# Part of a stream transpose moved from TensorE to VectorE and DMA, split one strip later

## The chip, the cores and the metric

The kernel runs on one core of one Trainium2 chip. The metric is the device time of one execution in microseconds (us), the median of several. The kernel before takes 2370.52 us (median of 3 runs, 2370.17 to 2370.91).

## The reference

Two layers of a causal decoder for 256 tokens with a stream `x` of width 2048, all in f32. Layer 0 has stick-breaking attention, layer 1 dilated window attention over shared keys and values; both have a gated ConvFFN and a gated embedding after it (called ple here):

```python
for i in range(DEPTH):                                  # DEPTH = 2
    h = rms_norm(x, attn_norm_w[i])
    x = x + (mixer_a(h, a_w_qkv, a_w_o) if i == 0 else mixer_b(h, b_w_q, b_w_o, shared K/V))
    x = x + conv_ffn(rms_norm(x, ffn_norm_w[i]), ffn_w_up[i], ffn_conv_w[i], ffn_conv_b[i], ffn_w_down[i])
    gate = sigmoid(rms_norm(x, ple_norm_w[i]) @ ple_w_gate[i])
    x = x + gate * (p[i] @ ple_w_proj[i])
return rms_norm(x, final_norm_w)
```

D_FF is 5632, the attention of layer 0 has 16 heads of 128, that of layer 1 has 12. The shared keys and values come from a norm of the stream between the layers.

## The kernel before

**Products.** Every f32 operand is split in two parts of fewer bits, high and low, and a product is three products: high by high, low by high, high by low. Weights come from memory in pieces of 4 blocks of 128x512 (`raw`, 1 MB, 4 buffers, loaded by SP's queue in order). ScalarE writes the high part of two blocks (`whi`, line 275), VectorE the low part (`wlo`, line 276); there are 4 buffers of each, so they run up to three pairs ahead of TensorE. Both are placed with a high priority.

**The stream** lies in `x[0]`, `x[1]`: 128 tokens each on the partitions, 2048 columns. It is treated in four strips `s` of 512 columns. Five stages end by adding to it strip by strip and preparing the next stage's operand, and are called the five parts here: the output projection of layer 0 (`wo_a`, 16 blocks per strip), the second half of its down projection (`wdn`), its ple, the output projection of layer 1 (`wo_b`, 12 blocks per strip), and the second half of its down projection. In each, TensorE makes a strip's two products of 128 tokens (`strip_v`, lines 317 to 319, tile `accv`), VectorE adds them to the strip (line 565, in ple line 660), and ScalarE squares the result for the next norm (line 212).

**The turn.** The next stage needs the strip with its columns on the partitions, as four blocks of 128x256. `turn(s)` has TensorE transpose it: 8 transposes of 128x128 by the identity (line 244) into two banks (`two`). Then `split_x` writes each block times the norm's gain as `h`: ScalarE the high half (line 140), VectorE the low half (line 141); ple keeps a plain copy too (`xT`, line 672). The first half of each down projection has no norm and no turn, nor has the last ple.

**The norm.** After strip 3 VectorE sums the squares, ScalarE takes ln and exp (lines 164, 165) and VectorE makes a diagonal matrix (`diag`, line 230), which TensorE multiplies by ones (`nrm`, line 232) to spread the factor over columns; after the down projections this last product is left out.

**Memory for the turn's results** comes from a ring of NRING tiles of 128x512, which `h`, `xT`, the FFN's products `g` and the attention's tiles share. The FFN has 11 pairs of up strips; `half` says how many are made, and multiplied by their rows of the down projection, before the rest.

**Order.** Each engine has one queue and takes its instructions in order. A scheduler lays them out at build time by the order of the program and by priorities; `tc.issue_after(i)` keeps what follows on an instruction's engine behind it. POOL (GpSimd) has no work in the program.

Of the kernel before, what the change touches and what calls it, by code (L numbers as in the profile page):

```python
# [10 lines left out]
F32 = mybir.dt.float32  # L11
# [3 lines left out]
AF = mybir.ActivationFunctionType  # L15
# [48 lines left out]

RAW = 4
WARM = 9
NRING, NRAW, NWSP = 42, 4, 4
AHEAD = 200
KV_AT = (0, 6, 12, 16)
PI_PARTS = _two_pi_parts()  # L70
# [3 lines left out]
def tile_trunk(ctx, tc, head_d, xT_d, x_d, pT_d, pos_d, vec_d, cst_d, csb_d, wqkv, wo_a, wkv, wq_b, wo_b, wup, wdn, wpg, wpp, gfin_d, out_d):  # L74
# [3 lines left out]
    wraw = ctx.enter_context(tc.tile_pool(name="wraw", bufs=NRAW))  # L78
    wsp = ctx.enter_context(tc.tile_pool(name="wsp", bufs=NWSP))
    tmp = ctx.enter_context(tc.tile_pool(name="tmp", bufs=3))  # L80
    psum = ctx.enter_context(tc.tile_pool(name="psum", bufs=8, space=bass.MemoryType.PSUM))

    uid = [0]
# [45 lines left out]
    def gain(base, j):  # L129
        return vec[:, base + j : base + j + 1]  # L130


    last = {}

    def split_x(src, j, bases):

        out = []
        for b in bases:
            h = rt("h", dt=F32R)
            last["split"] = nc.scalar.activation(h[:, :S], src, AF.Copy, scale=gain(b, j)).ins  # L140
            nc.vector.scalar_tensor_tensor(  # L141
                h[:, S:], src, gain(b, j), f32(h[:, :S]), op0=OP.mult, op1=OP.subtract
            )
            out.append(h)
        return out

# [4 lines left out]
    def strip_of(t, s):  # L151
        return x[t][:, s * 512 : (s + 1) * 512]
# [51 lines left out]
    class Norm:  # L204
# [4 lines left out]

        def add(self, s, t):  # L210
            q = tt("sq", (P, 768), tag="e", bufs=1)[:, :512]
            nc.scalar.activation(q, strip_of(t, s), AF.Square, accum_out=self.s[:, t, s : s + 1])  # L212

        def half(self, t):

# [20 lines left out]

    def turn(s):

        two = two_banks()
        out = [two[:, o // 2, (o % 2) * S : (o % 2 + 1) * S] for o in range(4)]  # L240
        for o, d in enumerate(out):
            for t in (1, 0):
                c = s * 512 + o * P
                nc.tensor.transpose(d[:, t * P : (t + 1) * P], x[t][:, c : c + P], idf)  # L244
        return two, out

    def weights(W, s, n, fine=False, before=lambda k0: None, block=None, base=0, ringed=0):

# [308 lines left out]
    def add_strips(W, xs, gain_of, norm, base=0):  # L557

        out = []
        for s in range(4):  # L560
            ps = strip_v(W, s, xs, base)
            if norm is not None and s == 3:
                norm.table = load_table()
            for t in range(2):
                nc.vector.tensor_tensor(strip_of(t, s), ps[t], strip_of(t, s), op=OP.add)
                if norm is not None:
                    norm.add(s, t)
            if norm is not None:
                for o, b in enumerate(turn(s)[1]):
                    out += split_x(b, 4 * s + o, [gain_of])  # L570
        return out

    def ffn(i, xs, rstd):
        cv = V_CONV + i * 4 * 2 * FB

        def conv(j, ps, y):
            col = lambda r: vec[:, cv + r * 2 * FB + j : cv + r * 2 * FB + j + 1]
            u = tt("u", tag="t", bufs=6)
            evac(ps, rstd, u)
            nc.scalar.activation(y, u, AF.Identity, scale=col(2), bias=col(3))  # L580
            nc.vector.scalar_tensor_tensor(y[:, 1:], u[:, : S - 1], col(1), y[:, 1:], op0=OP.mult, op1=OP.add)
            nc.vector.scalar_tensor_tensor(y[:, 2:], u[:, : S - 2], col(0), y[:, 2:], op0=OP.mult, op1=OP.add)

        def part(strips):
            gs = []
            for s in strips:
                ps = strip_t(wup[i], s, xs)
                gates = []
                for o in range(4):
                    y = tt("gate", bufs=4)  # L590
                    conv(4 * s + o, ps[o], y)
                    silu = nc.scalar.activation(y, y, AF.Silu).ins
                    gates.append(y)
                ps = strip_t(wup[i], FB // 4 + s, xs)
                for o in range(4):
                    y = tt("val", tag="t", bufs=6)
                    conv(FB + 4 * s + o, ps[o], y)
                    nc.vector.tensor_tensor(y, y, gates[o], op=OP.mult)
                    g = rt("g", dt=F32R)
                    split(y, g)  # L600
                    gs.append(g)
            return gs, silu

        half = (FB // 4 + 1) // 2
        gs, _ = part(range(half))
        add_strips(wdn[i], gs, None, None)
        gs, silu = part(range(half, FB // 4))
        if i == 0:
            rotary_tables(silu)
        norm = Norm()  # L610
        h = add_strips(wdn[i], gs, G_PLE + i * KB, norm, base=4 * half)
        return h, norm
# [23 lines left out]
    def ple(i, xs, ps_, rc, norm, gain_of=None):  # L636

        out, raw, gf = [], [], []
        if gain_of is None:
            for s in range(4):  # L640
                t = rt("gfin")
                nc.scalar.dma_start(
                    t, bass.AP(tensor=gfin_d.tensor, offset=gfin_d.offset + 512 * s, ap=[[0, P], [1, 512]])
                )
                gf.append(t)
        for s in range(4):
            end = gain_of is None and s == 3
            if end:
                pr = strip_v(wpp[i], s, ps_)
                gp = strip_v(wpg[i], s, xs, tail=KB, ringed=KB // 2)  # L650
            else:
                gp = strip_v(wpg[i], s, xs)
                pr = strip_v(wpp[i], s, ps_)
            for t in range(2):
                g = tt("pg", (P, 768), tag="w", bufs=2)[:, :512]
                nc.scalar.activation(g, gp[t], AF.Sigmoid, scale=rc[:, t : t + 1])
                if s == 3 and (end or t == 1):
                    norm.table = load_table()
                nc.vector.tensor_tensor(g, pr[t], g, op=OP.mult)
                nc.vector.tensor_tensor(strip_of(t, s), strip_of(t, s), g, op=OP.add)  # L660
                norm.add(s, t)
                if end:
                    finish(t, norm.half(t), gf[3])
                elif gain_of is None:
                    nc.vector.tensor_tensor(strip_of(t, s), strip_of(t, s), gf[s], op=OP.mult)
                if end and t == 0:
                    tc.keep_in_program_order(nc.scalar.preload_act_table_set("sigmoid_and_others"))
            if gain_of is not None:
                two, bs = turn(s)
                for o in range(0, 4, 2):  # L670
                    r = rt("xT")
                    nc.scalar.activation(r, two[:, o // 2], AF.Copy)
                    raw += [r[:, :S], r[:, S:]]
                    for q in range(2):
                        out += split_x(bs[o + q], 4 * s + o + q, [gain_of])
        return out, raw


# [137 lines left out]
```

## Time and profile before

| what | value |
|---|---|
| median of 3 runs | 2370.52 us |
| the profiled execution | 2371.05 us |
| its span | 2369.3 us, granted TensorE clock 0.998 |
| TensorE busy | 2355.6 us, 99% |
| VectorE busy | 1564.3 us, 66% |
| ScalarE busy | 1270.5 us, 54% |
| POOL busy | 0.2 us |
| the 16 DMA engines, mean busy share | about 0.53 |

The profile is one execution; the span is from its first to its last instruction, and 1.75 us lie around it. A busy TensorE is counted to the modelled end of each product, so products that overlap count as one; what a product costs in sequence is read from the chain that ended last, where a piece stands with the time by which it moved the chain on. A window's row gives, for a stretch of time, each engine's busy time with its number of instructions, the clock, the DMA engines' share and GB/s.

### The profile page before, as it was taken

The numbers are of one execution on the slowest core, as the hardware profiler recorded it, in microseconds if no ns is written. First come the engines' busy times: TensorE is split into PE (matmuls) and PEld (weight loads), VectorE is DVE, ScalarE is ACT, GpSimd is POOL, SyncE is SP. The second block draws the span as 40 slices with busy tenths as digits, with TensorE's granted clock in tenths as the row PEclk, the third lists the DMA queues.
The fourth block names the chain that finished last, engine by engine and source line by source line (L and its number), as shares of the span: only waits on it lengthen the run. The fifth ranks groups of instructions, "written<-read, shape, count | busy, mean of one in ns | idle before, by whom it ended". The sixth has DMA issues, their size and how long they took to land.

```text
span 2369.3 us, 31206 instructions
## 1 busy us (share of the span) xinstructions
PE 2355.6 (99%) x12258; PEld 2004.3 (85%) x12258; DVE 1564.3 (66%) x2377; ACT 1270.5 (54%) x1826; POOL 0.2 (0%) x4
## 2 busy tenths in 40 slices
PE   9999999999999999999999999999999999999998
PEld 7888888888888888888888888888888888888886
DVE  7566555778764578765567875677776457876555
ACT  6555545656543455654565444565654345555454
POOL 0000000000000000000000000000000000000000
PEclk9999999999999999999999999999999999999999
DMA  8455455555555555555555544555555555555553
GB/s 296 174 179 182 163 178 184 194 187 187 196 187 192 190 196 184 190 194 182 184 187 194 178 147 174 183 184 190 193 183 193 195 196 184 190 192 183 193 204 116
DMA packets 64852, 442.82 MB, mean 187 GB/s; under 512 B 7200, under 2 KB 7616, under 8 KB 12736
## 3 DMA queue, kind: packets, MB, share of 16 engines
q1 hardware_dynamic: 62352, 434.93, 52.8%
q10 hardware_dynamic: 2352, 5.88, 0.8%
q8 instruction: 96, 1.57, 0.3%
q14 instruction: 52, 0.43, 0.0%
HBM read 438.69 MB, written 2.10 MB: 186 GB/s over the span
## 4 chain that ended last, share of the span: by engine, by line
PE 99%; DVE 0%; ACT 0%; DMA 0%; issue 0%; SPq 0%; DVEq 0%
PE acc L302 36%; PE acc L305 18%; PE accv L319 14%; PE accv L317 14%; PE accv L318 14%; PE two L346 2%; PE two L244 1%; PE two L420 0%; DMA raw<-in_wqkv 0%; PE keys L346 0%; PE two L421 0%; ACT whi L275 0%; DVE wlo L276 0%; ACT sq L212 0%; PE nrm L232 0%
## 5 line engine op out<-in xcount | busy, mean ns | idle before, releaser
L276 DVE TENSOR_TENSOR wlo<-raw,whi 128x1024 fp32r<-128x1024 f32 (+1 forms) x821 | 1003.9, 1223 | 722.0 <-ACT whi L275 718.6
L275 ACT ACTIVATE whi<-raw 128x1024 fp32r<-128x1024 f32 (+1 forms) x821 | 868.2, 1058 | 881.7 <-PE accv L319 426.6
L302 PE MATMUL acc<-h,whi 128*128 128x512 f32 x3712 | 1167.0, 396 | 1.9 <-DVE h L141 1.6
L305 PEld LDWEIGHTS acc<-h,wlo 128*128 128x128 f32 x3712 | 697.1, 188 | 163.3
L305 PE MATMUL acc<-h,wlo 128*128 128x256 f32 x3712 | 731.0, 278 | 0.0
L302 PEld LDWEIGHTS acc<-h,whi 128*128 128x128 f32 x3712 | 567.1, 189 | 4.6 <-DVE h L141 1.9
L319 PE MATMUL accv<-whi,g 128*128 128x512 f32 x704 | 274.7, 390 | 0.0
L318 PE MATMUL accv<-wlo,g 128*128 128x512 f32 x704 | 274.2, 390 | 0.0
L317 PE MATMUL accv<-whi,g 128*128 128x512 f32 x704 | 274.1, 389 | 0.0
L317 PE MATMUL accv<-whi,h 128*128 128x512 f32 x464 | 181.8, 392 | 0.0
L319 PE MATMUL accv<-whi,h 128*128 128x512 f32 x464 | 181.4, 391 | 0.0
L318 PE MATMUL accv<-wlo,h 128*128 128x512 f32 x464 | 181.4, 391 | 0.0
L318 PEld LDWEIGHTS accv<-wlo,g 128*128 128x128 f32 x704 | 132.2, 188 | 27.4
L319 PEld LDWEIGHTS accv<-whi,g 128*128 128x128 f32 x704 | 132.2, 188 | 27.2
L317 PEld LDWEIGHTS accv<-whi,g 128*128 128x128 f32 x704 | 132.2, 188 | 27.1
L324 ACT ACTIVATE c<-acc 128x256 f32<-128x256 f32 x232 | 86.4, 374 | 33.4 <-PE acc L305 33.4
L319 PEld LDWEIGHTS accv<-whi,h 128*128 128x128 f32 x464 | 87.2, 188 | 18.0
L317 PEld LDWEIGHTS accv<-whi,h 128*128 128x128 f32 x464 | 87.2, 188 | 17.5
L318 PEld LDWEIGHTS accv<-wlo,h 128*128 128x128 f32 x464 | 87.2, 188 | 17.4
L325 DVE TENSOR_TENSOR c<-acc,c 128x256 f32<-128x256 f32 x232 | 92.2, 418 | 0.0
L319 PE MATMUL accv<-whi,o 128*128 128x512 f32 x224 | 88.0, 393 | 0.0
L318 PE MATMUL accv<-wlo,o 128*128 128x512 f32 x224 | 87.5, 391 | 0.0
(178 smaller groups left out, 1416.9 us busy)
## 6 DMA issues: line engine op xcount, KB each, us to landing
raw<-in_wup SPq DMA_DIRECT2D x176, 1024.0 KB, 4.8
raw<-in_wdn SPq DMA_DIRECT2D x88, 1024.0 KB, 4.8
raw<-in_wqkv SPq DMA_DIRECT2D x44, 1024.0 KB, 4.9
raw<-in_wpg SPq DMA_DIRECT2D x32, 1024.0 KB, 4.9
raw<-in_wkv SPq DMA_DIRECT2D x24, 1024.0 KB, 4.8
raw<-in_wo_a SPq DMA_DIRECT2D x16, 1024.0 KB, 4.8
raw<-in_wq_b SPq DMA_DIRECT2D x12, 1024.0 KB, 4.9
raw<-in_wo_b SPq DMA_DIRECT2D x12, 1024.0 KB, 4.9
```

The lines of the kernel that those rows point to most:

```text
L244: nc.tensor.transpose(d[:, t * P : (t + 1) * P], x[t][:, c : c + P], idf)
L275: last["high"] = nc.scalar.activation(hi[:, c], r, AF.Copy).ins
L276: nc.vector.tensor_tensor(lo[:, c], r, f32(hi[:, c]), op=OP.subtract)
L302: nc.tensor.matmul(ps[o], hi[:, c], xs[k], start=k == 0, stop=False)
L305: nc.tensor.matmul(ps[o][:, S:], lo[:, c], xs[k][:, :S], start=False, stop=k == n - 1)
L317: nc.tensor.matmul(ps[t], xl, hi, start=k == 0, stop=False)
L318: nc.tensor.matmul(ps[t], xh, lo, start=False, stop=False)
L319: nc.tensor.matmul(ps[t], xh, hi, start=False, stop=k == n - 1)
L324: last["copy"] = nc.scalar.activation(c, ps[:, S:], AF.Copy).ins
L325: last["sum"] = nc.vector.tensor_tensor(c, ps[:, :S], c, op=OP.add).ins
L346: run.append(nc.tensor.matmul(*args, skip_group_check=True, **kw).ins)
```

## The change

`turn(s)` no longer uses TensorE. VectorE transposes the strip's two tiles in blocks of 32x32 (line 250 of the new kernel) into ring tiles `y`. POOL's queue writes each to a tile in memory (`there`, 256 KB each), waits for both, and reads them back in four DMAs (line 257, 32 partitions each, pieces of 512 bytes) so that each block lies whole in `z` (name `turned`, one buffer in SBUF). `Turned.add` keeps strips 0 to 2 back: a strip's blocks are split only after the next strip has been added and squared. Strip 3 goes through `turn_at_once`, which is the old `turn`. The splits of strips 0 to 2 now read SBUF in place of PSUM, and ple's plain copies are 16 of 128x256 in place of 8 of 128x512. The ring has 40 tiles in place of 42, and `half` is 5 in place of 6, so that the first half of the down projection has 20 blocks and the second 24.

```diff
--- before.py
+++ after.py
@@ -64,7 +64,7 @@
 
 RAW = 4
 WARM = 9
-NRING, NRAW, NWSP = 42, 4, 4
+NRING, NRAW, NWSP = 40, 4, 4
 AHEAD = 200
 KV_AT = (0, 6, 12, 16)
 PI_PARTS = _two_pi_parts()
@@ -78,6 +78,7 @@
     wraw = ctx.enter_context(tc.tile_pool(name="wraw", bufs=NRAW))
     wsp = ctx.enter_context(tc.tile_pool(name="wsp", bufs=NWSP))
     tmp = ctx.enter_context(tc.tile_pool(name="tmp", bufs=3))
+    dram = ctx.enter_context(tc.tile_pool(name="dram", bufs=2, space=bass.MemoryType.DRAM))
     psum = ctx.enter_context(tc.tile_pool(name="psum", bufs=8, space=bass.MemoryType.PSUM))
 
     uid = [0]
@@ -132,15 +133,18 @@
 
     last = {}
 
+    def like(ap, src):
+        return ap.rearrange("p (a r) -> p a r", r=src.shape[2]) if len(src.shape) == 3 else ap
     def split_x(src, j, bases):
 
         out = []
         for b in bases:
             h = rt("h", dt=F32R)
-            last["split"] = nc.scalar.activation(h[:, :S], src, AF.Copy, scale=gain(b, j)).ins
-            nc.vector.scalar_tensor_tensor(
-                h[:, S:], src, gain(b, j), f32(h[:, :S]), op0=OP.mult, op1=OP.subtract
-            )
+            high, low = like(h[:, :S], src), like(h[:, S:], src)
+            last["split"] = nc.scalar.activation(high, src, AF.Copy, scale=gain(b, j)).ins
+            nc.vector.scalar_tensor_tensor(low, src, gain(b, j), f32(high), op0=OP.mult, op1=OP.subtract)
             out.append(h)
         return out
 
@@ -209,7 +213,8 @@
 
         def add(self, s, t):
             q = tt("sq", (P, 768), tag="e", bufs=1)[:, :512]
-            nc.scalar.activation(q, strip_of(t, s), AF.Square, accum_out=self.s[:, t, s : s + 1])
+            square = nc.scalar.activation(q, strip_of(t, s), AF.Square, accum_out=self.s[:, t, s : s + 1])
+            last["square"] = square.ins
 
         def half(self, t):
 
@@ -236,13 +241,47 @@
 
     def turn(s):
 
+        there = dram.tile([2 * P, 512], F32, tag="turn", name=nm("there"))
+        for t in range(2):
+            y = rt("y")
+            nc.vector.transpose(
+                y.rearrange("p (b o r) -> p o b r", b=4, o=4), strip_of(t, s).rearrange("p (o b c) -> p o b c", o=4, b=4)
+            )
+            nc.gpsimd.dma_start(there[t * P : (t + 1) * P], y)
+        z = tt("turned", (P, 8, 4, 32), bufs=1)
+        back = there.rearrange("(a c) (b f) -> b c a f", c=32, b=4)
+        for b in range(4):
+            nc.gpsimd.dma_start(z[32 * b : 32 * b + 32].rearrange("p a o r -> p a (o r)"), back[b])
+        return [z[:, :, o] for o in range(4)]
+    def turn_at_once(s):
         two = two_banks()
         out = [two[:, o // 2, (o % 2) * S : (o % 2 + 1) * S] for o in range(4)]
         for o, d in enumerate(out):
             for t in (1, 0):
                 c = s * 512 + o * P
                 nc.tensor.transpose(d[:, t * P : (t + 1) * P], x[t][:, c : c + P], idf)
-        return two, out
+        return out
+    class Turned:
+        def __init__(self, use):
+            self.use = use
+            self.strip = None
+        def add(self, s):
+            if self.strip is not None:
+                with tc.issue_after(last["square"]), tc.issue_after(last["added"]):
+                    self.use(*self.strip)
+            if s == 3:
+                self.use(s, turn_at_once(s))
+            else:
+                self.strip = (s, turn(s))
 
     def weights(W, s, n, fine=False, before=lambda k0: None, block=None, base=0, ringed=0):
 
@@ -557,17 +596,22 @@
     def add_strips(W, xs, gain_of, norm, base=0):
 
         out = []
+        def use(s, blocks):
+            for o, b in enumerate(blocks):
+                out.extend(split_x(b, 4 * s + o, [gain_of]))
+        turned = Turned(use)
         for s in range(4):
             ps = strip_v(W, s, xs, base)
             if norm is not None and s == 3:
                 norm.table = load_table()
             for t in range(2):
-                nc.vector.tensor_tensor(strip_of(t, s), ps[t], strip_of(t, s), op=OP.add)
+                last["added"] = nc.vector.tensor_tensor(strip_of(t, s), ps[t], strip_of(t, s), op=OP.add).ins
                 if norm is not None:
                     norm.add(s, t)
             if norm is not None:
-                for o, b in enumerate(turn(s)[1]):
-                    out += split_x(b, 4 * s + o, [gain_of])
+                turned.add(s)
         return out
 
     def ffn(i, xs, rstd):
@@ -601,7 +645,7 @@
                     gs.append(g)
             return gs, silu
 
-        half = (FB // 4 + 1) // 2
+        half = FB // 4 // 2
         gs, _ = part(range(half))
         add_strips(wdn[i], gs, None, None)
         gs, silu = part(range(half, FB // 4))
@@ -636,6 +680,17 @@
     def ple(i, xs, ps_, rc, norm, gain_of=None):
 
         out, raw, gf = [], [], []
+        def use(s, blocks):
+            for o, b in enumerate(blocks):
+                if o % 2 == 0:
+                    r = rt("xT")
+                d = r[:, o % 2 * S : (o % 2 + 1) * S]
+                nc.scalar.activation(like(d, b), b, AF.Copy)
+                raw.append(d)
+                out.extend(split_x(b, 4 * s + o, [gain_of]))
+        turned = Turned(use)
         if gain_of is None:
             for s in range(4):
                 t = rt("gfin")
@@ -657,7 +712,7 @@
                 if s == 3 and (end or t == 1):
                     norm.table = load_table()
                 nc.vector.tensor_tensor(g, pr[t], g, op=OP.mult)
-                nc.vector.tensor_tensor(strip_of(t, s), strip_of(t, s), g, op=OP.add)
+                last["added"] = nc.vector.tensor_tensor(strip_of(t, s), strip_of(t, s), g, op=OP.add).ins
                 norm.add(s, t)
                 if end:
                     finish(t, norm.half(t), gf[3])
@@ -666,13 +721,7 @@
                 if end and t == 0:
                     tc.keep_in_program_order(nc.scalar.preload_act_table_set("sigmoid_and_others"))
             if gain_of is not None:
-                two, bs = turn(s)
-                for o in range(0, 4, 2):
-                    r = rt("xT")
-                    nc.scalar.activation(r, two[:, o // 2], AF.Copy)
-                    raw += [r[:, :S], r[:, S:]]
-                    for q in range(2):
-                        out += split_x(bs[o + q], 4 * s + o + q, [gain_of])
+                turned.add(s)
         return out, raw
 
 
```

TensorE's queue at the start of `wo_a`'s strip 1, before (accv: the products; o: attention's output; x, idf: the transposes' operands):

```order
L317 MATMUL accv_2783<-whi_2779,o_784 128x512 [waits Activation_49]
L318 MATMUL accv_2783<-wlo_2780,o_784 128x512 [waits DVE_49]
L319 MATMUL accv_2783<-whi_2779,o_784 128x512
L317 MATMUL accv_2783<-whi_2779,o_787 128x512
L318 MATMUL accv_2783<-wlo_2780,o_787 128x512
L244 MATMUL two_2756<-idf,x_75 128x128 [waits DMAHW3_49,DMAHW2_49,DVE_49]
L244 MATMUL two_2756<-idf,x_74 128x128 [waits DMAHW5_49]
```

and now:

```order
L356 MATMUL accv_2776<-whi_2772,o_786 128x512 [waits Activation_49]
L357 MATMUL accv_2776<-wlo_2773,o_786 128x512 [waits DVE_49]
L358 MATMUL accv_2776<-whi_2772,o_786 128x512
L356 MATMUL accv_2776<-whi_2772,o_789 128x512
L357 MATMUL accv_2776<-wlo_2773,o_789 128x512
L358 MATMUL accv_2776<-whi_2772,o_789 128x512
L356 MATMUL accv_2783<-whi_2772,o_786 128x512
```

Eight transposes (two are shown) stood between the fifth product and the sixth and waited for VectorE's additions; they are gone. In the whole queue 12012 products and transposes stand where there were 12132.

ScalarE's queue in `wo_b` where strip 2 has just been added, before (sq: the squares; h: the splits; whi: the weights' high parts):

```order
L212 ACTIVATE sq_12928,ssum_12560<-x_74 128x512 [waits DVE_49]
L212 ACTIVATE sq_12931,ssum_12560<-x_75 128x512 [waits DVE_49,Activation_49]
L140 ACTIVATE h_12942<-two_12933,vec 128x256 [waits PE_49]
L140 ACTIVATE h_12945<-two_12933,vec 128x256 [waits DVE_49]
L275 ACTIVATE whi_13026<-raw_13024 128x1024 [waits DMAHW4_49,PE_49]
L140 ACTIVATE h_12948<-two_12933,vec 128x256 [waits DVE_49]
L275 ACTIVATE whi_13042<-raw_13024 128x1024 [waits PE_49]
```

and now:

```order
L216 ACTIVATE sq_12959,ssum_12597<-x_76 128x512 [waits DVE_49]
L216 ACTIVATE sq_12962,ssum_12597<-x_77 128x512 [waits DVE_49,Activation_49]
L314 ACTIVATE whi_13060<-raw_13058 128x1024 [waits DMAHW4_49,PE_49]
L146 ACTIVATE h_12964<-turned_12849,vec 128x256 [waits DMASW6_49,DMASW7_49,DMASW1_49,DMASW0_49]
L146 ACTIVATE h_12967<-turned_12849,vec 128x256
L146 ACTIVATE h_12970<-turned_12849,vec 128x256
L146 ACTIVATE h_12973<-turned_12849,vec 128x256
L314 ACTIVATE whi_13076<-raw_13058 128x1024 [waits PE_49]
```

The splits are now those of strip 1, their first waits for four DMAs of POOL's queue in place of TensorE, and the last `whi` of strip 3's weights stands behind them all.

ScalarE's queue where `wo_a` ends, before (n: ln and exp of the norm; two: strip 3's blocks):

```order
L212 ACTIVATE sq_3247,ssum_2611<-x_74 128x512 [waits DVE_49]
L212 ACTIVATE sq_3250,ssum_2611<-x_75 128x512 [waits DVE_49,Activation_49]
L140 ACTIVATE h_3261<-two_3252,vec 128x256 [waits PE_49]
L164 ACTIVATE n_3275<-rcol_3273 128x2 [waits DVE_49]
L165 ACTIVATE n_3275<-n_3275 128x2 [waits Activation_49]
L140 ACTIVATE h_3264<-two_3252,vec 128x256 [waits DVE_49]
```

and now:

```order
L216 ACTIVATE sq_3246,ssum_2613<-x_76 128x512 [waits DVE_49]
L216 ACTIVATE sq_3249,ssum_2613<-x_77 128x512 [waits DVE_49,Activation_49]
L146 ACTIVATE h_3251<-turned_3101,vec 128x256 [waits DMASW6_49,DMASW7_49,DMASW1_49,DMASW0_49]
L146 ACTIVATE h_3254<-turned_3101,vec 128x256
L146 ACTIVATE h_3257<-turned_3101,vec 128x256
L314 ACTIVATE whi_3399<-raw_3397 128x1024 [waits DMAHW6_49,PE_49]
L146 ACTIVATE h_3260<-turned_3101,vec 128x256
L146 ACTIVATE h_3272<-two_3263,vec 128x256
L168 ACTIVATE n_3286<-rcol_3284 128x2 [waits DVE_49]
L169 ACTIVATE n_3286<-n_3286 128x2 [waits Activation_49]
```

Strip 2's four splits and one `whi` now stand ahead of the norm's ln and exp. The product `nrm` that waits for this norm stands on TensorE's queue behind 38 products of the next stage where it stood behind 22. At the end of `wo_b` the order is the other way round: ln and exp stand right behind the squares, ahead of strip 2's splits, and `nrm` stands behind 19 products where it stood behind 22. At the end of layer 0's ple the splits stand ahead, and 46 products lie between strip 3's transposes and `nrm` where 18 lay.

POOL's queue had no rows of the program; now it has six DMAs for each of the 15 turns of strips 0 to 2. The two writes wait for VectorE's transposes; the first of the four reads waits for both writes, and for ScalarE to be done with the blocks that `turned` held before.

## The prediction

> **What bounds the kernel now.** I read the page first, then the chain that ended last, in order of time, then the busy time of each engine in the stretch with the shortest strips, then the DMA issues and the waits. The page:
>
> ```profile
> span 2369.3 us, 31206 instructions
> PE 2355.6 (99%) x12258; PEld 2004.3 (85%) x12258; DVE 1564.3 (66%) x2377; ACT 1270.5 (54%) x1826; POOL 0.2 (0%) x4
> PEclk9999999999999999999999999999999999999999
> PE 99%; DVE 0%; ACT 0%; DMA 0%; issue 0%; SPq 0%; DVEq 0%
> PE acc L302 36%; PE acc L305 18%; PE accv L319 14%; PE accv L317 14%; PE accv L318 14%; PE two L346 2%; PE two L244 1%; PE two L420 0%; DMA raw<-in_wqkv 0%; PE keys L346 0%; PE two L421 0%; ACT whi L275 0%; DVE wlo L276 0%; ACT sq L212 0%; PE nrm L232 0%
> ```
>
> TensorE is the chain from end to end at its full clock. Nothing else ends a wait that matters, so what TensorE no longer does comes off the time, as long as nothing new makes it wait. The transposes (L244) are 1% of the chain. In order of time the chain shows each group of eight (start us, us by which it moved the chain on); I quote one row for each of the five parts and all three of ple, whose rows differ:
>
> ```profile
> 331.39 0.87 PE two L244 x8
> 1049.23 0.87 PE two L244 x8
> 1161.67 0.88 PE two L244 x8
> 1186.62 0.99 PE two L244 x8
> 1212.14 0.98 PE two L244 x8
> 1475.42 0.90 PE two L244 x8
> 1492.69 0.90 PE two L244 x8
> 2177.06 0.87 PE two L244 x8
> ```
>
> **The change: what leaves TensorE.** Of 20 groups, 15 go. The other two strips of `wo_a` and of both down projections read 0.87 like the row shown, and `wo_b`'s third 0.90. The sum is 3 x 0.87 + 3 x 0.87 + (0.88 + 0.99 + 0.98) + 3 x 0.90 + 3 x 0.87 = 13.4 us. The timeline has a group's modelled length, which overlaps its neighbours:
>
> ```profile
> 1049.06 1.04 PE L244 MATMUL two<-idf,x 128*128 128x128 f32 x8
> ```
>
> So 15 x 1.04 = 15.6 us bounds the gain from above. I take 13.4, because the chain counts what the next product really waits.
>
> **What VectorE gets.** Thirty transposes of 128x512, SBUF to SBUF. No such row exists. The nearest are an addition of the same size with both inputs in SBUF, the fastest instruction of that size, and a shuffle beside an arithmetic instruction of its size:
>
> ```profile
> L660 DVE TENSOR_TENSOR x<-x,pg 128x512 f32<-128x512 f32 x16 | 10.9, 686 | 0.1
> L633 DVE TENSOR_SCALAR x<-x,rhalf 128x512 f32<-128x512 f32 x4 | 1.8, 482 | 0.1
> L401 DVE STREAM_SHUFFLE sw<-qk 32x256 f32<-32x256 f32 x24 | 9.9, 434 | 0.0
> L402 DVE TENSOR_TENSOR sw<-sw,rot 32x256 f32<-32x256 f32 x24 | 9.7, 404 | 0.0
> L276 DVE TENSOR_TENSOR wlo<-raw,whi 128x1024 fp32r<-128x1024 f32 x819 | 1002.5, 1224 | 722.0 <-ACT whi L275 718.6
> ```
>
> A shuffle costs what arithmetic does, so I take 0.69 us each, 21 us in all. The bounds are 0.48 us, and twice 0.686, 1.37 us, if the data passes twice. All of it lies beside TensorE if VectorE has room in the shortest strips, those of `wo_b`. The windows (length, TensorE, weight loads, VectorE, ScalarE, POOL, clock, DMA share, GB/s):
>
> ```profile
> 1475.00:1492.00 17.00, 17.00 (x80) 14.06 (x79) 10.05 (x13) 8.89 (x15) 0.00 (x0) 1.00 0.53 181
> ```
>
> 10.05 + 2 x 0.69 = 11.4 us (12.8 at the upper bound) in a strip that will last 17.27 - 0.90 = 16.4 us: room, so no cost. If that cover went, the lateness would show as TensorE waiting for `wlo`.
>
> **What ScalarE gets.** 60 splits read SBUF and not PSUM, and ple copies 16 small blocks for 8 large ones:
>
> ```profile
> L140 ACT ACTIVATE h<-two,vec 128x256 fp32r<-128x256 f32 x80 | 37.1, 464 | 10.2 <-DVE h L141 10.0
> L140 ACT ACTIVATE h<-x,vec 128x256 fp32r<-128x256 f32 x14 | 6.3, 495 | 0.0
> L672 ACT ACTIVATE xT<-two 128x512 f32<-128x512 f32 x8 | 4.7, 590 | 0.4 <-PE two L244 0.3
> L148 ACT ACTIVATE p<-pin 128x256 fp32r<-128x256 f32 x4 | 1.4, 400 | 0.0
> ```
>
> 60 x 0.031 + 16 x 0.400 - 8 x 0.590 = 3.5 us more, beside TensorE in an engine busy 8.9 us of 17. No cost. `half` 5 for 6 and the shorter ring leave the number of products as it is; a ring tile that is not yet free only stops `g`, which follows the last product of the strip anyway. No cost either.
>
> **The trip through memory.** This is the new wait: ScalarE's first split of a strip waits for four DMAs, and behind it in its queue stand `whi` rows that TensorE needs. I set a budget at `wo_b`. T is the end of a strip. VectorE then has 3 `wlo`, 4 low halves and 2 transposes in its row order, 3 x 1.224 + 4 x 0.482 + 2 x 0.69 = 7.0 us, with some 0.7 us of waiting for ScalarE T + 7.7. ScalarE asks for the blocks no earlier than after the next strip's squares, about T + 18, so a trip of 10 us holds nobody up. The last `whi` of strip 3 stands behind the splits. TensorE wants it five pairs into that strip (a pair is 12 products of 0.227, 2.72 us), at T + 16.4 + 13.6 = T + 30, and 4 splits, a `whi` and a `wlo` take 4.3 us. So TensorE waits only if the trip is longer than 30 - 4.3 - 7.7 = 18 us. The other parts' strips are longer: `wo_a` 22.7 us (23 us of trip allowed), ple 25.5 (26), `wdn` 28.1 (29). No DMA of POOL's is in this trace; the nearest rows are those of the other queues with the same 256 KB, and the time that SP needs to issue one (ns, min/median/max):
>
> ```profile
> out<-x SPq DMA_DIRECT2D x4, 256.0 KB, 2.7
> out<-x ACTq DMA_DIRECT2D x4, 256.0 KB, 3.0
> pin<-in_pT ACTq DMA_DIRECT2D x2, 256.0 KB, 2.6
> x<-in_xT SPq DMA_DIRECT2D x7, 256.0 KB, 6.6
> L634 SPq DMA_DIRECT2D out<-x x4: 332/360/415, 2353.2 to 2364.4; - x4
> ```
>
> Lower bound: write 2.7, read 2.6, five issues of 0.36: 7.1 us. Upper: 3.0 + 6.6 + five issues that each first wait for a running `wlo`, 5 x (0.36 + 1.22): 17.5 us. I take about 9.5 (2.7 + 5.0 + 1.8), as the write is the very shape of `out`. Within the bounds it costs TensorE nothing. [...]
>
> **The traffic.** Each turn writes and reads 0.52 MB, 15.7 MB in all, in 256 pieces of 2 KB and 1024 of 512 bytes:
>
> ```profile
> DMA packets 64852, 442.82 MB, mean 187 GB/s; under 512 B 7200, under 2 KB 7616, under 8 KB 12736
> q10 hardware_dynamic: 2352, 5.88, 0.8%
> ```
>
> A packet of q10 (2.5 KB on average) takes 0.008 x 16 x 2369 / 2352 = 0.129 us. At that price a turn takes 1280 x 0.129 / 16 = 10.3 us of each DMA engine, where `wo_b` leaves 0.47 x 17.2 = 8.1 us free and the other parts 10.6 or more; ours average 0.8 KB, so I take two thirds of it, which fits everywhere. No cost; late next would be the loads of `raw`.
>
> **The ends of the parts.** The wait there is of the norm's product:
>
> ```profile
> PEld nrm L232 <- DVE diag L230: 1.0, 2, 0.5
> ```
>
> At the end of `wo_a` four splits (2.0 us) and a `whi` (1.06) now stand ahead of ln and exp, and `nrm` stands 16 products later (8 of 0.23, 8 of 0.12: 2.8 us). The wait grows by 0.3 us. In ple's end 28 products more cover the longer chain, and at `wo_b`'s end the chain comes first, as before. Cost: 0.3 us, from 0 to 1.
>
> **The sum** against the profiled execution: 2371.05 - 13.4 + 0.3 = 2357.9. The median lies 0.53 us under that execution: **2357.4 us**.
>
> **Rivals.** (a) *The trip is late and the kernel slower.* Above 18 us TensorE waits in two strips of `wo_b`, above 23 in two of `wo_a`, above 26 in ple. At 24 us, 2 x 6 + 2 x 1 = 14 us eat the gain; at 26 us, 16 + 6 = 22 us make 2379. For it: POOL's issues are in no row, and VectorE, busy 59% here, may hold them up. Against: even with a whole `wlo` ahead of each issue the trip is 17.5 us. [...]
>
> (b) *The gain is hidden.* TensorE would wait for loads instead. This needs 0.143 us a packet: 11.4 us a turn, 3 x 3.3 in `wo_b`, 3 x 0.8 in `wo_a`, 12.5 us together, and 2370. For it: more than a thousand small packets a turn. Against: 0.129 us for packets three times as large, and four `raw` buffers of 5.4 us each in front.
>
> (c) *The norm's wait takes its place*: 3.1 us at each of three ends, if the splits go ahead and TensorE's queue gives no cover, 2357.4 + 9 = 2366. Against: the order covers 2.8 and 4.9 us at two and puts the chain first at the third.
>
> **Chances.** Forecast 0.68; (a) 0.12, of which 0.10 slower than before; (b) 0.10; (c) 0.10. A measurement can tell 0.2% (4.7 us) from no change. Faster: 0.68 + 0.10 + 0.02 = 0.80; within 0.2%: 0.10; slower: 0.10. The range goes from the bound of 15.6 us with the norm's waits gone (2354) to rival (c) (2366).
>
> **What would show it.** Right: the first-half strips of `wo_b` 16.3 to 16.4 us apart in the chain, 5 groups of eight transposes left, no row of TensorE waiting for `whi` or `wlo`, VectorE's transposes near 0.69 us and busy time up by 21, `h` never waiting for a DMA of `turned`. Wrong: `whi` or `h` of ScalarE waiting for `turned`, TensorE idle behind it in `wo_b`; `raw` landing much later than 4.9 us; `nrm` waiting several us; or a longer time around the span, 1.75 us now, from one more queue.

## The result and the profile after

The changed kernel takes 2358.26 us (median of 4 runs, 2357.20 to 2358.42), the kernel before 2370.72 in the same comparison (4 runs, 2370.17 to 2370.92). The ratio is 0.9947, 95% interval 0.9930 to 0.9964. That is 12.5 us less; the forecast was 13.1. The profiled execution took 2358.29 us, so 1.8 us lie outside its span, as before.

The page of the changed kernel: span, busy time of the engines, share of the chain.

```profile
span 2356.5 us, 31193 instructions
PE 2342.1 (99%) x12138; PEld 1992.0 (85%) x12138; DVE 1578.5 (67%) x2407; ACT 1270.9 (54%) x1834; POOL 52.4 (2%) x94
PE 98%; DVE 1%; ACT 0%; DMA 0%; issue 0%; SPq 0%; DVEq 0%; ACTq 0%
```

TensorE lost 120 instructions (15 groups of 8) and 2355.6 - 2342.1 = 13.5 us of busy time. Its idle time went from 2369.3 - 2355.6 = 13.7 us to 2356.5 - 2342.1 = 14.4. So the span is 13.5 - 0.7 = 12.8 us shorter. TensorE is still the chain from end to end.

The added work and what is left of the old, by line (count, busy us, mean ns, idle time ahead and what ended it), and then from the page the DMAs (count, KB each, median us from issue to landing) and POOL's queue (packets, MB, share of 16 engines):

```profile
L250 DVE STREAM_TRANSPOSE y<-x 128x512 f32<-128x512 f32 x30 | 21.1, 702 | 0.0
L146 ACT ACTIVATE h<-turned,vec 128x256 fp32r<-128x256 f32 x60 | 27.1, 495 | 7.4 <-DMA turned<-there 7.4
L267 PE MATMUL two<-idf,x 128*128 128x128 f32 x40 | 5.2, 273 | 0.0
```

```profile
there<-y POOLq DMA_DIRECT2D x30, 256.0 KB, 3.9
turned<-there POOLq DMA_DIRECT2D x60, 128.0 KB, 4.5
raw<-in_wo_b SPq DMA_DIRECT2D x12, 1024.0 KB, 4.8
q0 software_dynamic: 5280, 15.73, 2.3%
```

A VectorE transpose takes 0.70 us. Five groups of TensorE transposes are left. ScalarE did wait for `turned`, 7.4 us in all. The loads of `raw` land as early as before (4.8 us).

Where ScalarE waited is read from `wo_b`, strip by strip. First VectorE (start us, us; the additions L610 start when a strip's products end), then POOL, then ScalarE (in brackets the idle time ahead and what ended it):

```profile
1482.01 1.28 DVE L610 TENSOR_TENSOR x<-accv,x 128x512 f32<-128x512 f32 x2
1490.38 0.70 DVE L250 STREAM_TRANSPOSE y<-x 128x512 f32<-128x512 f32 x1
1498.33 1.28 DVE L610 TENSOR_TENSOR x<-accv,x 128x512 f32<-128x512 f32 x2
1509.09 0.70 DVE L250 STREAM_TRANSPOSE y<-x 128x512 f32<-128x512 f32 x1
1514.65 1.28 DVE L610 TENSOR_TENSOR x<-accv,x 128x512 f32<-128x512 f32 x2
```

```profile
1491.37 0.56 POOL L253 DMA_DIRECT2D there<-y  x1 [1.16 <-DVE y L250]
1497.67 2.34 POOL L257 DMA_DIRECT2D turned<-there  x4 [5.75 <-ACT whi L314]
```

```profile
1505.21 1.71 ACT L146 ACTIVATE h<-turned,vec 128x256 fp32r<-128x256 f32 x4 [2.62 <-DMA turned<-there]
1524.39 1.71 ACT L146 ACTIVATE h<-turned,vec 128x256 fp32r<-128x256 f32 x4 [4.77 <-DMA turned<-there]
```

The strips are 16.3 us apart. The second strip ended at 1482.0. Its second transpose ended at 1491.1 (9.1 us later), its splits began at 1505.2: a trip of 14.1 us. It is made of 0.3 us to the issue, 0.56 of issue, 5.7 until POOL goes on to the reads (it waits for the second write's landing; the `whi` that the row names has no part in the trip), 2.34 for four issues, and 5.2 until the last landing. Why the second write took 5.7 us shows in SP's queue. A load of weights of 1 MB was issued 0.9 us ahead of it:

```profile
1490.48 5.57 SPq L297 DMA_DIRECT2D raw<-in_wup  x2
```

The `wlo` between the two transposes frees a `raw` buffer, and the load that then starts landed at 1496.4, the write at 1497.1. The median of 3.9 us above hides this: outside ple the first writes of a trip landed in 2.4 to 2.7 us (one in 3.7), and the second ones, each 0.9 us behind a load, in 5.0 to 6.8.

The third strip's second transpose ended 11.5 us after the strip, since in VectorE's order they stand behind the low halves, and these waited for the late splits. Its splits began 26.1 us after the strip.

Waits of the norm's product:

```profile
PEld nrm L237 <- DVE diag L235: 1.3, 3, 0.6
PE nrm L237 <- DVE diag L235: 0.3, 1, 0.3
```

### The profile page after: what moved, and what is told of

It is laid out like the page before. It is cut to its first block, busy times and chain, and to the rows that moved or that the text cites. A ratio compares the mean times of both kernels' runs of the same rounds, so it can differ in the third digit from the quotient of the medians.

```text
span 2356.5 us, 31193 instructions
## 1 busy us (share of the span) xinstructions
PE 2342.1 (99%) x12138; PEld 1992.0 (85%) x12138; DVE 1578.5 (67%) x2407; ACT 1270.9 (54%) x1834; POOL 52.4 (2%) x94
## 3 DMA queue, kind: packets, MB, share of 16 engines
q0 software_dynamic: 5280, 15.73, 2.3%
## 4 chain that ended last, share of the span: by engine, by line
PE 98%; DVE 1%; ACT 0%; DMA 0%; issue 0%; SPq 0%; DVEq 0%; ACTq 0%
PE acc L341 36%; PE acc L344 18%; PE accv L357 14%; PE accv L356 14%; PE accv L358 14%; PE two L385 2%; PE two L459 0%; DVE wlo L315 0%; DMA raw<-in_wqkv 0%; ACT whi L314 0%; PE keys L385 0%; PE two L460 0%; ACT sq L216 0%; PE two L267 0%; PE nrm L237 0%
```

## The experiments

Each ratio is against runs of the kernel before on the same chip. Its medians were 2370.40 (first four runs), 2370.45 (next four) and 2370.64 (last three).

### Only the removal, only the addition

`no_trip`: the changed kernel, `turn` returns the stream strip itself.

```
     def turn(s):
-        there = dram.tile(...)
...
-        return [z[:, :, o] for o in range(4)]
+        return [strip_of(o // 2, s)[:, (o % 2) * S : (o % 2 + 1) * S] for o in range(4)]
```

> Left out: the trip, and with it the transposing of the first three strips of each part. The splits read the stream strips as they stand, one strip later as in the changed kernel; VectorE's 30 transposes and POOL's 90 DMAs are gone. Theory (what leaves TensorE is the whole gain and the added work is hidden): the time of the changed kernel, 2358.3 us, within 0.5 us, with the same waits for the norm. Rival (the added work costs something, so the gain came out 0.6 us below the forecast): 2357.4 or less.

Measured: 2356.54 us (2356.15 to 2358.94), ratio 0.9942 (0.9929 to 0.9956). That is 13.9 us less than before, where the forecast had 13.4 leaving TensorE. By the letter the rival won: without the trip the kernel is faster than with it. How much is best read beside `hop1` (below), measured on the same chip and the changed kernel in all but one DMA that delays nobody: 2357.38, so 0.8 us. When the starts of the same TensorE products are compared in the traces of the changed kernel and of `no_trip`, 0.6 us of the difference arises between 1519 and 1541 us, around the end of `wo_b`, and 0.5 us in the program's first 15 us, where other pairs of executions differ by as much. So the added work costs 0.6 to 0.8 us, and its place is the end of `wo_b`, where the forecast had only "as before". It is not the trip alone: in `no_trip` the scheduler also put the norm's product there later in TensorE's queue (1522.6 us against 1519.9).

`work_alone`: the kernel before with all its TensorE transposes, and `turn`'s new body beside them, its result unread.

```
     def turn(s):
+        if s < 3:
+            ship(s)
         two = two_banks()
```

> The kernel before with all of its TensorE transposes, and the added work beside them with nobody reading its result: 30 VectorE transposes, 90 DMAs of POOL's queue, the ring of 40 tiles and the down projection's halves as in the changed kernel. Theory (VectorE, the DMA engines and POOL have room): 2370.7 us, the time before, within 0.7 us. Rival of contention (a tenth of the packets' price and late loads): up to 2380; each DMA issue stretched by VectorE would show as a landing and an issue time longer than in the changed kernel.

Measured: 2370.65 us (2370.42 to 2371.53), ratio 1.0002 (0.9993 to 1.0010). Its page and DMA rows:

```profile
PE 2355.9 (99%) x12258; PEld 2003.8 (85%) x12258; DVE 1577.7 (67%) x2407; ACT 1271.3 (54%) x1826; POOL 52.4 (2%) x94
there<-y POOLq DMA_DIRECT2D x30, 256.0 KB, 4.3
turned<-there POOLq DMA_DIRECT2D x60, 128.0 KB, 5.7
```

VectorE's 30 transposes, 16 MB written and read back, and POOL's 90 DMAs cost nothing when nobody waits for them. The removal alone gives the gain; the traffic does not take it back. Rival (b) falls.

### A longer trip

`hop1` and `hop2` put one or two small DMAs between writes and reads; `far1` one that needs the second write. TensorE's order is the same in all three as in the changed kernel; in `far1` a `whi` and its `wlo` changed places with splits in two spots of `wo_b`.

```
+        for _ in range(2):       # hop1: 1
+            nc.gpsimd.dma_start(z[:1, 0], there[:1, :P]...)
...
+            nc.gpsimd.dma_start(z[:1], there[2 * P - 2 :]...)   # far1
         for b in range(4):
             nc.gpsimd.dma_start(z[32 * b : 32 * b + 32]..., back[b])
```

> The changed kernel, with one small DMA (512 bytes, memory to the first row of turned) put between the writes and the reads of each trip, so that the trip is longer by one DMA's latency and nothing else moves. The trip measured from the end of the second transpose to the first split is 14.1 us in wo_b's second strip; with some 4 us more it is 18, the edge of the budget that the prediction gave (18 us). Theory: 2358.3 to 2360 us, TensorE waiting at most 1 us in a strip of wo_b. If the budget was too generous (splits that come late make the next trip later, since VectorE's transposes stand behind the low halves): 2362 or more already.

Measured: 2357.38 us (2357.08 to 2357.76). The dose was almost none: the small DMA reads the first write's rows and runs while the second write lands, and the splits of `wo_b`'s second strip begin at 1505.01 (1505.21 in the changed kernel). Only 2 of the 15 trips got clearly longer (by 3.3 and 7.3 us, in `wo_a` and ple), and nobody waited for these.

> The same with two such DMAs one after the other: a trip of some 22 us. By the prediction's budget TensorE waits 4 us in each of two strips of wo_b and nowhere else (wo_a has 23 us, ple 26, the down projections 29): 2366 us. If the lateness is handed on from strip to strip: 2370 or more, with waits in wo_a too. If TensorE has more in hand than the budget says: 2358.3.

Measured: 2363.57 us (2362.02 to 2367.42), 6.2 us above `hop1`. ScalarE's waits, and those of TensorE, between 1500 and 1545 us (total, times, longest):

```profile
ACT h L146 <- DMA turned<-there: 13.7, 2, 7.1
PE two L269 <- DVE x L612: 1.9, 1, 1.9
```

The splits of the second strip begin at 1509.30, 17.6 us behind its second transpose: 3.5 us more than in the changed kernel, not 8, because only the last of the four reads waited for the small DMAs. TensorE does not wait for `whi` in the strips, where the budget put the loss; once, in the fourth strip of `wo_b`, it waits 0.6 us for a `wlo`. It waits for VectorE's addition `x` at the end of `wo_b`, which stands behind the low halves and transposes of the strip before, for the norm at the end of `wo_a` (1.3 us), and some 25 us into the next part for a `c` (1.8 us).

> The changed kernel with one small DMA (4 KB) between writes and reads that needs the second write, so that every read comes one landing later. A trip of 14.1 us from the end of the second transpose to the first split becomes about 19. By the prediction's budget (18 us) TensorE waits 1 us in each of two strips of wo_b: 2360 us. By the budget corrected with the traces (blocks are asked for on the way at 9 and 11 us behind the strip's end and not 7.7, and each late strip makes the next one later) some 3 to 5 us in each of wo_b's strips and nothing elsewhere: 2367 to 2374.

Measured: 2362.95 us (2362.34 to 2365.52). In `wo_b` the trip grew by less than meant: it is 15.1 and 15.8 us against 14.1 and 14.6. At the third strip of `wo_a` it grew by more: the last read landed 16.2 us after the second transpose, against 12.9 in the changed kernel. The span is 4.7 us longer. By the starts of the same products, 3.6 us are lost at the end of `wo_a` and 2.3 at the end of `wo_b`, and 1.2 were gained in the program's first 15 us, ahead of any turn. POOL's reads of that strip and the first of ScalarE's splits of it, in the changed kernel:

```profile
388.61 2.35 POOL L257 DMA_DIRECT2D turned<-there  x4 [5.27 <-ACT whi L314]
398.01 1.30 ACT L146 ACTIVATE h<-turned,vec 128x256 fp32r<-128x256 f32 x3
```

The last read landed at 395.4, so 2.6 us were in hand. The same in `far1` (the last two reads), with ScalarE's ln and exp (`n`), which stand behind these splits:

```profile
392.56 1.16 POOL L259 DMA_DIRECT2D turned<-there  x2 [2.14 <-DMA turned<-there]
398.78 1.31 ACT L146 ACTIVATE h<-turned,vec 128x256 fp32r<-128x256 f32 x3 [1.93 <-DMA turned<-there]
401.70 0.19 ACT L168 ACTIVATE n<-rcol 128x2 f32<-128x2 f32 x1
401.92 0.20 ACT L169 ACTIVATE n<-n 128x2 f32<-128x2 f32 x1
```

The trip was 3.3 us longer, and it began 1.2 us later after the strip's end, because the splits before it had waited 1.1 us. So ScalarE waited 3.3 + 1.2 - 2.6 = 1.9 us, and TensorE behind it. TensorE's wait, and the windows (length, then busy time and instructions of TensorE, weight loads, VectorE, ScalarE, POOL, then the granted clock, DMA share and GB/s):

```profile
PE nrm L237 <- DVE diag L235: 2.1, 1, 2.1
```

```profile
401.44:404.85 3.41, 1.29 (x7) 0.80 (x6) 3.31 (x9) 2.07 (x5) 0.00 (x0) 1.00 0.00 0
404.85:408.26 3.41, 3.41 (x12) 2.88 (x11) 1.22 (x3) 1.85 (x4) 0.00 (x0) 0.50 0.49 175
```

TensorE waited 2.1 us for the norm, and then worked for 3.4 us at half its clock.

So lateness is paid first at the ends of the parts, through the norm and the last addition, and hardly in the strips.

### An earlier start, and none held back

`early`: VectorE's transposes with a high priority, to stand right behind the additions.

```
-            nc.vector.transpose(...)
+            with tc.high_priority(offset=AHEAD):
+                nc.vector.transpose(...)
```

> The changed kernel with VectorE's two transposes put right behind the strip's additions instead of behind three wlo and four low halves. TensorE's order stays but for one product, ScalarE's order stays but for the last part of wo_b. The trip then begins some 3 us after the strip's end and not 9 to 11, the blocks are there at 17 us, and ScalarE never waits for turned. Theory (the trip's lateness costs 0.6 us at the end of wo_b and nothing else): 2357.4 to 2357.9, that is 0.5 to 1 us less than the changed kernel. Rival (VectorE's wlo, two transposes later, make TensorE wait at each strip's start): 2360 or more.

Measured: 2357.21 us (2357.11 to 2358.15), ratio 0.9943 (0.9929 to 0.9956). The waits and DMAs:

```profile
ACT h L146 <- DMA turned<-there: 0.7, 1, 0.7
PE nrm L237 <- DVE diag L235: 0.9, 1, 0.9
```

```profile
there<-y POOLq DMA_DIRECT2D x30, 256.0 KB, 2.7
```

ScalarE's wait fell from 7.4 to 0.7 us, nearly as expected, though the transposes did not come as early as meant: in `wo_b` the second one ends 7.1 us after the strip, where 3 were expected and 9.1 and 11.5 had been. The median landing of a write is 2.7 us and not 3.9: the two transposes now follow each other without a `wlo` between them, so both writes go out ahead of the next load in most trips, and 10 of the 15 second writes landed in 2.6 to 3.0 us. But at the end of `wo_b` two splits and a `wlo` now stand ahead of the norm's ln, and its product waits 0.9 us there. The gain over the changed kernel (0.1 us by the two spans, 0.8 by the medians, each against its own runs of before) is not separated from nothing by these intervals.

`soon`: no strip is held back.

```
-                self.strip = (s, turn(s))
+                self.use(s, turn(s))
```

> The changed kernel without holding a strip back: the splits of a strip's blocks are issued after its own turn. ScalarE asks for them behind some six whi of the next strip, about 11 us after the strip's end, and they come at 23 us; TensorE has four pairs of whi in hand, some 11 us. Theory (one strip later is what hides the trip): TensorE waits about 5 us in each of 15 strips, 2400 to 2450 us. Rival (the trip would be hidden anyway): 2359 or less.

Measured: 2365.62 us, with a wide spread (10 runs, 2357.58 to 2378.34), ratio 0.9983 (0.9969 to 0.9997). The expectation missed by 34 us at least. The scheduler itself puts the splits behind five `whi` of the next strip (four in ple). ScalarE then waits only 0.9 to 5.8 us at a time (29.7 us in 12 places), where the expectation had 12, and four pairs of `whi` are in hand. So its waits reach TensorE in one place only, again the norm at the end of `wo_b`:

```profile
PE nrm L237 <- DVE diag L235: 4.7, 1, 4.7
```

```profile
1524.95:1528.37 3.42, 0.81 (x6) 0.45 (x4) 2.90 (x6) 3.08 (x8) 0.00 (x0) 1.00 0.00 0
1528.37:1531.78 3.41, 1.33 (x4) 1.15 (x5) 3.15 (x9) 1.49 (x3) 0.00 (x0) 0.50 0.60 195
```

So holding a strip back is worth some 7 us here, with less spread; it is not what hides the trip in the strips.

### Another queue

`sp`: `nc.sync` for `nc.gpsimd` in `turn`.

> The changed kernel with the six DMAs of each turn issued by SP and not by POOL, between SP's loads of weights. Theory (POOL's issues are not starved by VectorE): the landings are as with POOL, 3 to 4 us a write and 4 to 5 us a read, SP issues in about 0.36 us instead of 0.57, the trip is some 2 us shorter, and the loads queued behind the waiting reads come 5 us later, which the four raw tiles cover: 2357 to 2359 us. [...] Second rival (the loads behind the reads come too late): 2365 or more, TensorE waiting for whi.

Measured: 2360.81 us (2359.52 to 2361.13), ratio 0.9958 (0.9944 to 0.9971). Its DMAs, and SP's reads in its queue:

```profile
there<-y SPq DMA_DIRECT2D x30, 256.0 KB, 4.0
turned<-there SPq DMA_DIRECT2D x60, 128.0 KB, 5.4
```

```profile
1517.99 1.82 SPq L257 DMA_DIRECT2D turned<-there  x4
```

SP's landings are no shorter than POOL's (3.9 and 4.5). So nothing shows that VectorE, busy 67%, holds back what POOL issues, which was an argument for rival (a). From the second transpose to the last landing the trips of `wo_b` take 13.5 and 12.4 us, against 14.1 and 14.5 with POOL: shorter, as expected. Still `sp` is slower than the changed kernel by about 2.6 us. Its trace loses them in one place, where TensorE waits for `h` of the third strip; ScalarE's rows show why:

```profile
PE acc L341 <- DVE h L147: 2.6, 1, 2.6
```

```profile
1527.73 1.06 ACT L314 ACTIVATE whi<-raw 128x1024 fp32r<-128x1024 f32 x1 [1.72 <-PE acc L341]
1528.69 1.69 ACT L146 ACTIVATE h<-turned,vec 128x256 fp32r<-128x256 f32 x4
```

The blocks had landed at 1525.2. In this run the scheduler put three more `whi` ahead of these splits, and the last of them waits for TensorE itself. So the loss is one of order on ScalarE, not of the queue's landings.

### The last strips too

`all4`: as `early`, and strip 3 goes through memory in every part. `best`: only in the two down projections, with the norm's arithmetic ahead at the end of `wo_b`; `early_norm` is `best` without the last strips. The cut is from `best`; `all4` has no such conditions.

```
-                self.use(s, turn_at_once(s))
+                self.use(s, turn(s) if self.last else turn_at_once(s))
...
+            with tc.high_priority(offset=AHEAD) if ahead else ExitStack():
                 nc.vector.reduce_sum(rc, self.s, axis=mybir.AxisListType.X)
```

> As the run with early transposes, and the last strip of each part goes through memory too: no transposes on TensorE are left. Five groups of 0.87 to 1.04 us leave, 4.6 us. The last strip's blocks are there 17 us after its end, its splits done at 19; TensorE comes to block 12 of the next part's first strip some 17 us after. Theory: it waits 1 to 2 us at most at each of the five ends, and the time is 2354 to 2358.5. Rival (the trip is 14 us only in the mean, and the next part's wlo and splits stand behind it): waits of 5 us, 2370 or more.

Measured: 2364.45 us (2362.52 to 2366.74), ratio 0.9973 (0.9962 to 0.9985). The 4.6 us left and more came back. The costliest place is the end of ple, 6.6 us by the starts of the same products, where the granted clock is 0.50 again, from within one wait of 3.6 us on:

```profile
PE acc L341 <- DVE h L147: 3.6, 1, 3.6
```

```profile
1243.04:1246.45 3.41, 1.46 (x6) 0.62 (x5) 1.23 (x1) 0.39 (x1) 0.59 (x1) 1.00 0.85 180
1246.45:1249.87 3.42, 1.05 (x3) 0.86 (x4) 1.16 (x3) 2.44 (x8) 0.00 (x0) 0.50 0.64 268
```

> As the run with early transposes, but at the end of wo_b the norm's arithmetic (sum, logarithm, exponential, diagonal) is put ahead of two of the four splits and of a wlo that stood before it there. The early run lost 1.3 us against the changed kernel at that one place, where the norm's product waits. Theory: some 0.5 to 1 us of it comes back, 2356.3 to 2357. Rival (the place does not matter, the difference between these runs is the program's start): 2357.2 as the early run.

Measured: 2357.93 us (2357.86 to 2358.48), ratio 0.9947 (0.9934 to 0.9961). At the end of `wo_b` its trace gains 0.5 us on that of `early`, the lower end of what was expected, but its median is 0.7 us longer. The expectation of the time is not borne out; the place is too small to be seen in it.

> As the run before, and the last strip of the two down projections goes through memory too, while wo_a, ple and wo_b keep TensorE for their last strip. Where all last strips went, these two ends alone lost nothing: 0.91 and 0.80 us left TensorE and no wait came, since ple begins with two strips' products per pair and its first strip asks for block 12 late. Theory: 1.7 us less than the early_norm run, 2354.6 to 2355.4, the fastest of all. Rival (the trip at the end of a down projection collides with ple's loads): no change or slower.

Measured: 2357.02 us (2356.35 to 2360.92), ratio 0.9946 (0.9934 to 0.9959). Its median is the lowest of the complete kernels, but by less than these runs tell apart. In its profiled execution (2360.92 us, its slowest) the norm at the end of `wo_b` was late:

```profile
PE nrm L238 <- DVE diag L236: 2.6, 1, 2.6
```

```profile
1522.53:1525.94 3.41, 1.24 (x7) 1.11 (x8) 3.41 (x6) 2.30 (x5) 0.00 (x0) 1.00 0.00 0
1525.94:1529.35 3.41, 3.41 (x13) 2.83 (x12) 0.71 (x2) 1.55 (x3) 0.00 (x0) 0.50 0.79 238
```

Nor was the end of the first down projection free in that execution: ple's first products waited 1.4 us for an `h`. So what the last strips give is put at risk at the part's end: `early`, `best` and the changed kernel stand within 1.2 us of each other.

## Why the prediction came out right, and where it was wrong

**What leaves TensorE: right.** 13.4 us by the chain; the busy time fell by 13.5, and `no_trip` took 13.9 us less. The chain's rows were the right measure, and the modelled length of the timeline (15.6) was too long.

**VectorE and ScalarE: right.** 0.69 us a transpose was forecast and 0.70 measured, 495 ns a split from SBUF forecast and measured, and no cost where the result is unread (`work_alone`). VectorE's busy time rose by 14.2 us and not by 21: its other instructions took 4.6 us less together in this execution, and overlaps with neighbours count once.

**The traffic: right in the outcome, wrong in the count.** The 5280 packets of q0 are 352 a turn and not 1280 (256 of 4096 bytes and 96 of 4); pieces of 512 bytes did not stand as packets of their own. A packet took 0.023 x 16 x 2356.5 / 5280 = 0.164 us, so a turn took 352 x 0.164 / 16 = 3.6 us of each DMA engine, a third of the 10.3 that the prediction bounded. A packet's price was above the 0.143 us from which rival (b) was to decide; the rival failed by the number of packets.

**The trip: the step that was mis-sized.** The forecast was 9.5 us, the measurement 14.1 and 14.6, inside the bounds of 7.1 to 17.5. The write's landing was put at 2.7 us, from writes at the program's end, and took 5.7 until POOL went on, because a load of 1 MB stood ahead of the second write; the first writes did land in about 2.5. The five issues took 0.56 and 0.59 us each, 2.9 together, where SP's 0.36 had given 1.8. The reads' 5.0 was close (5.2).

**The budget: wrong, and by luck without effect.** It gave 18 us and a margin of 8.5. Its start was T + 7.7; it was 9.1 and 11.5. The sum left out the strip's own two additions (1.28 us), which stand first on VectorE, and a late split makes the next strip's transposes late, which the prediction had not followed around. And it asked the wrong wait: it followed ScalarE's `whi` to TensorE, while lateness first reaches TensorE through the norm's ln and exp and through VectorE's last addition, at the ends of the parts. There little was in hand: 2.6 us at the end of `wo_a`, and none in `wo_b`, where the trip was already waited for. Trips 3.3 and 1.1 us longer lost 3.6 and 2.3 us at these two places (`far1`). "`h` never waiting for `turned`" was wrong too: 7.4 us, hidden.

**The norm: sign right, place wrong.** 0.3 us at the end of `wo_a` was forecast and `wo_b` left unchanged. TensorE's idle time grew by 0.7 us. Its waits for the norm show no growth at the end of `wo_a` and some 0.4 us at the end of `wo_b`. This 0.4 us more, and 0.5 us by which the forecast was moved from the profiled execution to the median (here both are the same), are the 0.9 us by which 2357.4 missed.

**The rivals.** That VectorE holds up POOL's issues, which (a) thought possible, did not show: POOL's DMAs landed in 3.9 and 4.5 us, SP's in `sp` in 4.0 and 5.4. But a trip that is late does cost, from some 15 us on in `wo_b` and not from 18, and hardly in the strips. (b) is excluded by `work_alone`. (c), the norm's wait in the place of the one removed, is the one that `hop2`, `far1`, `soon` and `best` ran into. It had 0.10.

## What to carry to other kernels

What the critical engine no longer does comes off the time as the chain counts it, if its replacement lies on engines with room and someone checks what stands behind the replacement's wait in each queue. Follow that wait to the next norm or reduction at the end of a part as well as to the next operand in the steady state: it is at the ends that little was in hand here. And follow a late buffer once around the loop, since it starts the next trip later. Before a landing time is taken from another row, look at what is in flight there and here.

## What the runs showed of the hardware

**In four runs the granted clock was halved around a wait of TensorE of 2.1 to 4.7 us; in two, with 1.9 and 2.6 us, it was not.** After waits of 2.1 us (`far1`) and 2.6 (`best`) it was 0.50 for 3.41 us, and from within waits of 3.6 us (`all4`) and 4.7 (`soon`) on for 6.83. So `far1` lost 3.6 us by a wait of 2.1. But around the 1.9 us of `hop2` and the 2.6 us of `sp` it stayed at 1.00. By the rows above TensorE stood idle 2.0 us (`all4`), 2.1 (`far1`), 2.2 (`best`) and 2.6 (`soon`) of the 3.41 us ahead of the fall. Here are 3.41 us of `hop2` that hold most of its wait:

```profile
1517.62:1521.03 3.41, 1.91 (x15) 1.83 (x16) 2.87 (x7) 1.86 (x6) 0.00 (x0) 1.00 0.98 404
```

And two stretches as long over which the wait of `sp` is spread:

```profile
1526.20:1529.61 3.41, 1.72 (x11) 1.34 (x9) 1.85 (x2) 1.88 (x4) 0.00 (x0) 1.00 0.66 267
1529.61:1533.03 3.42, 2.54 (x14) 2.23 (x15) 2.87 (x7) 1.61 (x4) 0.00 (x0) 1.00 0.53 172
```

They hold 1.5, 1.7 and 0.9 us of idle time. So in these runs the length of a wait alone does not tell whether the clock falls: after 2.1 us in `far1` it did, around 2.6 in `sp` it did not. What else decides was not shown; a 3.41 us stretch laid otherwise over `sp` would hold its whole wait.

**POOL's DMAs were dearer to issue here, not slower to land.** An issue took 0.56 to 0.59 us on POOL (one 0.71); on SP (`sp`) a write took 0.33 and four reads 1.82, 0.46 each. Landings were no longer on POOL (medians 3.9 and 4.5 us, against 4.0 and 5.4).

**A write issued right behind a load landed right behind it.** Outside ple the same 256 KB write took 2.5 us as the first of a trip (median) and 5.0 us or more as the second, 0.9 us behind a 1 MB load of weights; 10 of these 12 landed 0.6 to 0.7 us after the load and two 1.9 us after it. Issued right behind the first, ahead of the load, it took 2.6 to 3.0 us in 10 trips of `early`.
